# A two-layer hybrid mixer network on one core: a list schedule that books the SBUF port, with priorities for each part of each mixer

## The chip, the core and the metric

The kernel runs on one core of a Trainium2 chip. The engines have short names in the rows: PE is TensorE (matmuls), PEld its weight loads, DVE is VectorE, ACT is ScalarE, POOL is GpSimd, SP is SyncE, on whose queue all transfers are issued. The metric is the device time of one execution in microseconds.

## What is computed

One inference step of a two-layer network on 384 tokens of width 1024 (128 context tokens and 256 latent tokens, which share the weights). Each layer is a half-step feed-forward block, a mixer and a second half-step feed-forward block:

```
x += 1/2 * gate1 * SwiGLU(adaLN1(RMSNorm(x)))
x += gate2 * W_out[ RWKV7 | windowed GQA+sink | gated DeltaNet ](W_in adaLN2(RMSNorm(x)))
x += 1/2 * gate3 * SwiGLU(adaLN3(RMSNorm(x)))
```

The mixer projects the normed tokens with W_in and hands the columns to three branches: RWKV7, a linear recurrence with a low-rank decay (in both directions), attention over a window of 128 with a sink and a cached context, and gated DeltaNet, a second recurrence in both directions, behind a convolution over 5 tokens:

```
S = (S * w_t[:, :, None, :]
     + jnp.einsum('bhvk,bhk->bhv', S, a_t)[..., None] * b_t[:, :, None, :]
     + v_t[..., None] * k_t[:, :, None, :])
```

Both recurrences are computed in chunks, which needs the inverse of a triangular matrix for each chunk, head and direction. Outputs are the tokens, the new keys and values, and the final states of both recurrences.

## The kernel before

**How the work is tiled.** Activations stand with channels on the 128 partitions and the 384 tokens (386 with two columns for the norm's shift) along the free axis. Every large product has float32 weights split in two: `split_w` (L940) writes whi on ScalarE and the rest wlo = wr − whi on VectorE, and `mm3` (L952) issues three matmuls of 128x128 by 128x386 for each pair. The feed-forward products are pg, pu and po, the mixer's input projections are pw (`project`, L1060: a product, then `evac`, which reads it out of PSUM with rstd into pg and on into prj); the mixer's output projection w_out is called po as well (po2 in the code, shown as po in the trace).

**The mixer** (L1037) is written in parts, each with a label: prR (projections of the RWKV branch), preR (decays and scan inputs kr, kt, bt, and the products lr), inv0 (the inverse for RWKV), prD (projections and convolution cv of the delta branch), gates, unit, prA (projections of attention), lev0 (assembling larger blocks of the inverse), preD, inv1 (the inverse for the delta branch), lev1, attnp and attn0 to attn2, and the scans scR and scD, for two groups of heads, three chunks and two directions each. A scan step is a short chain between PE, ScalarE and VectorE (yu, U, sd, btk, pd, ks). At the end of a scan comes a norm over heads (its mean is bm) and a product with a gate, which gives y, the input of the output projection.

`stage_inv` (L1299) works through 31 columns; each is a product `pr = R * Z` and a subtraction `Z -= pr` on 112 partitions, so a chain of 62 operations in a row, which may stand on VectorE or on GpSimd. Their widths go from 31 up to 256 and down again.

**What sets the order.** Nothing is issued as it is written. A `Recorder` (L198) notes every operation with what it depends on. `estimate` (L376) gives each a duration, `order` (L426) then plays the program through: whenever an engine is free, the ready operation with the highest priority goes. The priority `cp` is the longest way to the end of the program in modelled time, plus a bias by label from `BIAS`, plus 5000 for an accumulation that has begun. Operations recorded by `any`, `tt`, `copy`, `scale` or `fill` have several engines to choose from (`alts`); an engine that is free passes such an operation when another would have it done over 60 ns sooner, by the model. On PE, an operation whose weight tile has another shape than the last is put off as long as one of the same shape is at most `near` less urgent. Where the modelled PE would not be dense enough, the planner emits a filler, a 128x128 matmul on zeros (idle_ps, L706). `issue` (L695) then writes the operations in that order; most rows of the trace bear its line, L718. The order on each engine is fixed from there on; at run time an engine waits in that order for what it needs.

Of the kernel before, what the change touches and what calls it, by code (L numbers as in the profile page):

```python
# [36 lines left out]
SIDE = ("vvvvv", "mmm", "vvvv", "vvvv", "", "")  # L37

ROOM = {"kA": "h", "kS": "h", "vt": "h", "pt": "h", "ev": "h", "w0b": "h", "lora": "h", "yb": "r"}
TUNE = {'near': 2000.0, 'ahead': 8000.0, 'ahead2': 8000.0, 'finish': 5000.0, 'clock': True, 'dummy': 53.5, 'd1': 3600.0, 'd2': 7000.0}  # L40

BIAS = {'ada02': -100000.0, 'ada03': -100000.0, 'ada04': -100000.0, 'ada05': -100000.0, 'ada06': -100000.0, 'ada07': 0.0, 'ada08': 0.0, 'ada10': 0.0, 'ada11': -100000.0, 'ada12': -100000.0, 'ada13': -100000.0, 'ada14': -100000.0, 'ada15': -100000.0, 'ada16': -100000.0, 'ada17': -100000.0, 'ada18': -100000.0}
PLACES = {"u": 30, "r": 3, "w": 6, "a": 3, "b": 2, "h": 5, "t": 10, "ps": 7, "mxs": 2, "dram_ada": 2, "dram_s1": 2, "dram_s2": 2, "dram_s3": 2, "s4": 6}


# [123 lines left out]
class Op:  # L169
    __slots__ = ("eng", "meth", "args", "kw", "cost", "lat", "preds", "succs", "bufs", "idx", "cp", "need", "ready",  # L170
                 "start", "end", "tset", "label", "group", "seed", "filler", "follows", "pos", "held", "stall", "dma", "alts", "done",
                 "name", "real", "parts", "seq", "lead", "mode", "out")


class _Eng:
# [22 lines left out]
class Recorder:  # L198
# [91 lines left out]
    def any(self, *choices):  # L290

        op = self.add(*choices[0][:2], (), choices[0][2])
        op.alts = {}
        for eng, meth, kw in choices:
            op.eng, op.meth, op.kw = eng, meth, kw
            self.estimate(op)
            op.alts[eng] = (meth, kw, op.cost, op.lat, op.tset)
        self.choose(op, min(op.alts, key=lambda e: op.alts[e][2]))
        return op

    def choose(self, op, e):
        op.eng = e
        op.meth, op.kw, op.cost, op.lat, op.tset = op.alts[e]

    def copy(self, out, in_, pool=True):
        c = [("scalar", "copy", dict(out=out, in_=in_)), ("vector", "tensor_copy", dict(out=out, in_=in_))]
# [69 lines left out]
    def estimate(self, op):  # L376
# [4 lines left out]
        views = [v for v in list(a) + list(kw.values()) if isinstance(v, View)]  # L381
        ps = any(v.buf.tag in PSUM for v in views)
        sc = sum(isinstance(kw.get(k), View) for k in ("scalar", "scalar1", "scalar2", "bias", "scale", "accum_out"))
        op.tset, op.dma = None, 0.0
        e, m = op.eng, op.meth
        if m == "dma_start":
            nbytes = n * out.shape[0] * 4
            run = min(v.shape[-1] for v in (out, kw["in_"])) * 4
# [2 lines left out]
        elif e == "tensor":  # L391
            op.lat = 200.0
            op.seq = [self.product(*p) for p in op.parts]
            op.held = sum(p[3] for p in op.seq)
            op.cost = self.stream(0.0, op.seq, [0.0] * 16, 1.0)[1]
            op.mode, op.out = op.seq[0][4], op.seq[-1][4]
        elif e == "vector":
            if m == "tensor_reduce":
                n = int(np.prod(kw["in_"].shape[1:]))
            if m == "reciprocal":  # L400
                n *= 6
            full = ps or m in ("stream_shuffle", "tensor_reduce", "reciprocal") or any(k in kw for k in ("in1", "data"))
            op.cost = (65 + (n if full else n / 2)) / 0.96 + 62 * sc
            if m == "memset":
                op.cost = 8 + n
            op.lat = 130.0
        elif e == "scalar":
            op.cost = ((61 if isinstance(kw["in_"], View) and kw["in_"].buf.tag in PSUM else 112) + n) / 1.2 + 93 * sc
            op.tset = TSETS.get(kw.get("func"))
            op.lat = 142.0  # L410
        else:
            op.cost = 130 + n * (4.3 if sc else 3.3)
            if m == "memset":
                op.cost = 35 + n * 0.83
            elif m == "tensor_tensor":
                op.cost = 150 + n * 2.1
            elif m == "scalar_tensor_tensor":
                op.cost = 95 + n * 1.39
            op.lat = 120.0

    def wait(self, op, o):
        if op.eng == "tensor" and o.eng == "tensor":
# [3 lines left out]
    def order(self):  # L426
# [79 lines left out]
        def enter(op):  # L506
# [4 lines left out]
            else:  # L511
                heapq.heappush(gated, (op.pos - (self.ahead2 if op.follows else self.ahead), op.idx))

        win, busy, over, warm, ndum, past, dens, colt = 0, 0.0, 0.0, False, 0, [], 0.0, [0.0] * 16
        mode, nsw = (P, P), 0
        bus, tset, now, out, emit, wake, stuck = 0.0, None, 0.0, [], [], [], False
        for op in ops:
            if op.need == 0:
                enter(op)
        while len(out) < len(ops):  # L520
# [10 lines left out]
            for e in engs:  # L531
# [6 lines left out]
                while avail[e]:  # L538
# [15 lines left out]
                        op.stall = tag  # L554
                        continue
                    if op.alts:
                        here, best = now + op.alts[e][2], 1e18
                        for f in op.alts:
                            if f != e:
                                queue = sum(ops[x[1]].cost for x in avail[f] if x < item and not ops[x[1]].done)  # L560
                                best = min(best, max(free[f], now) + queue + op.alts[f][2])
                        if best < here - 60:
                            passed.append(item)
                            continue
# [86 lines left out]
                if op.tset and op.tset != tset:  # L651
                    tset = op.tset
                    cost += 1300.0
                op.start = now
                free[e] = now + cost
                if e != "tensor":
# [1249 lines left out]
```

## Time and profile before

| | us |
|---|---|
| median of 3 runs (1887.55 to 1890.82) | 1888.9 |
| profiled execution | 1892.28 |
| its span | 1890.5 |

| engine | busy us | share of the span |
|---|---|---|
| PE | 1842.2 | 97% |
| DVE | 1336.9 | 71% |
| ACT | 856.4 | 45% |
| POOL | 206.2 | 11% |

The page gives for the chain of work that ended last: PE 82% of the span, DVE 8%, ACT 4%, POOL 2%, DMA 2%. In time, the span is: feed-forward block to 345 us, first mixer (mixer 0) to 660, two feed-forward blocks to 1255, second mixer (mixer 1) from 1280 to 1575, feed-forward block to the end. A row of a timeline groups neighbouring instructions of one form (x4); its first number is the start in us from the start of the span, its second the duration, and a bracket gives the idle time before it and what ended it. PEclk is the clock granted to PE as a share of full speed.

### The profile page before, as it was taken

Reading aid. Unit: us, or ns where it says so; the run is one execution under the profiler, and the core shown is the slowest. Engines: PE = TensorE matmul, PEld = TensorE weight load, DVE = VectorE, ACT = ScalarE, POOL = GpSimd, SP = SyncE. Lnnn points to the kernel's source line nnn. Section 1 sums busy time; section 2 is a strip of 40 time slices with the busy share of each in tenths; the row PEclk is TensorE's granted clock in tenths of the full one; section 3 lists DMA queues with packets and bytes.
Section 4 is the critical chain, followed back from the end, with each engine's and each line's share of the span. In section 5 each row is a group of like instructions: output and inputs, shape, how many; then the busy total and the mean of one; then the engine's idle time right before and its main releaser. Section 6 shows DMA issues by size and latency. Waiting matters only on the chain.

```text
span 1890.5 us, 34461 instructions
## 1 busy us (share of the span) xinstructions
PE 1842.2 (97%) x13589; PEld 1690.1 (89%) x13589; DVE 1336.9 (71%) x2680; ACT 856.4 (45%) x1777; POOL 206.2 (11%) x322
## 2 busy tenths in 40 slices
PE   8999999989999999999999999998899999999998
PEld 6999999778766799999999999997686679999998
DVE  3999954886775679995459995458879646555444
ACT  4444433657445454443344443347664444434323
POOL 0000000251320200000000000014525011000000
PEclk9999999999899999999999999999999999999999
DMA  9566644365421255664455664443341213434442
GB/s 363 200 222 230 241 137 164 124 196 157 109 46 39 78 205 203 216 241 126 125 201 206 214 243 126 126 137 91 79 102 42 66 52 101 123 123 123 128 123 84
DMA packets 144033, 279.46 MB, mean 148 GB/s; under 512 B 50192, under 2 KB 76880, under 8 KB 143872
## 3 DMA queue, kind: packets, MB, share of 16 engines
q1 hardware_dynamic: 143872, 277.26, 46.1%
q8 instruction: 107, 1.75, 0.4%
q14 instruction: 54, 0.44, 0.1%
HBM read 264.80 MB, written 11.89 MB: 146 GB/s over the span
## 4 chain that ended last, share of the span: by engine, by line
PE 82%; DVE 8%; ACT 4%; POOL 2%; DMA 2%; issue 1%; SPq 0%; DVEq 0%; ACTq 0%; POOLq 0%
PE po L718 23%; PE pg L718 20%; PE pu L718 20%; PE pw L718 5%; PE idle_ps L706 3%; POOL pr L718 1%; ACT L714 1%; POOL Z L718 1%; PE q L718 1%; PE z L718 1%; DVE mxs L718 1%; PE gram L718 1%; PE pr L718 1%; PE aps L718 1%; PE sc L718 1%
## 5 line engine op out<-in xcount | busy, mean ns | idle before, releaser
L718 DVE TENSOR_TENSOR wlo<-wr,whi 128x1024 fp32r<-128x1024 f32 (+2 forms) x334 | 400.8, 1203 | 90.4 <-ACT whi L718 90.1
L718 ACT CAST whi<-wr 128x1024 fp32r<-128x1024 f32 (+2 forms) x334 | 339.7, 1019 | 174.4 <-PE po L718 84.4
L718 PE MATMUL pg<-xs,whi 128*128 128x386 f32 x1408 | 366.3, 341 | 0.2 <-POOL xs L718 0.2
L718 PE MATMUL pu<-xs,whi 128*128 128x386 f32 x1408 | 365.8, 341 | 0.0
L718 PE MATMUL po<-h,whi 128*128 128x384 f32 x1408 | 360.1, 337 | 0.0
L718 PEld LDWEIGHTS pg<-xs,whi 128*128 128x128 f32 x1408 | 257.4, 189 | 0.9 <-POOL xs L718 0.5
L718 PEld LDWEIGHTS pu<-xs,whi 128*128 128x128 f32 x1408 | 257.4, 189 | 0.0
L718 DVE CUSTOM_DVE_ANT_0 unread<-arow,crow 128x1024 bf16<-128x1024 f32 x208 | 253.8, 1220 | 3.0 <-ACT crow L718 1.1
L718 PEld LDWEIGHTS po<-h,whi 128*128 128x128 f32 x1408 | 255.7, 188 | 0.0
L718 PE MATMUL pu<-xs,wlo 128*128 128x386 f32 x704 | 238.8, 339 | 0.6 <-DVE wlo L718 0.6
L718 PE MATMUL pg<-xs,wlo 128*128 128x386 f32 x704 | 238.7, 339 | 0.0
L718 PE MATMUL po<-h,wlo 128*128 128x384 f32 x704 | 237.4, 337 | 0.0
L718 PE MATMUL pw<-xs,whi 128*128 128x386 f32 (+1 forms) x736 | 198.4, 350 | 9.8 <-ACT whi L718 7.1
L718 DVE SCALAR_TENSOR_TENSOR xT<-po,mods,xT 128x256 f32<-128x256 f32 (+1 forms) x96 | 35.3, 413 | 169.4 <-PE po L718 169.2
L718 PEld LDWEIGHTS pw<-xs,whi 128*128 128x128 f32 (+1 forms) x736 | 131.7, 186 | 21.3 <-ACT whi L718 8.6
L718 PE MATMUL pw<-xs,wlo 128*128 128x386 f32 (+1 forms) x368 | 128.4, 350 | 7.8 <-DVE wlo L718 7.6
L718 PEld LDWEIGHTS pu<-xs,wlo 128*128 128x128 f32 x704 | 134.1, 190 | 1.1 <-DVE wlo L718 1.1
L718 PEld LDWEIGHTS pg<-xs,wlo 128*128 128x128 f32 x704 | 134.1, 190 | 0.5 <-DVE wlo L718 0.4
L718 PEld LDWEIGHTS po<-h,wlo 128*128 128x128 f32 x704 | 132.1, 188 | 0.0
L706 PEld LDWEIGHTS <-idle_z 128*128 128x128 bf16 x1553 | 96.1, 100 | 33.2 <-issue 26.6
L706 PE MATMUL idle_ps<-idle_z 128*128 128x128 bf16 x1553 | 123.4, 224 | 0.0
L718 ACT CAST h<-up 128x384 fp32r<-128x384 f32 x88 | 45.2, 514 | 151.0 <-DVE up L718 151.0
(363 smaller groups left out, 2466.1 us busy)
## 6 DMA issues: line engine op xcount, KB each, us to landing
wr<-in_ffn_in SPq DMA_DIRECT2D x176, 512.0 KB, 4.5
arow<-in_adat SPq DMA_DIRECT2D x104, 512.0 KB, 3.6
wr<-in_ffn_out SPq DMA_DIRECT2D x64, 512.0 KB, 3.7
wr<-in_w_in SPq DMA_DIRECT2D x44, 512.0 KB, 4.5
wr<-in_ffn_out SPq DMA_DIRECT2D x32, 384.0 KB, 3.3
araw<-in_ada SPq DMA_DIRECT2D x24, 512.0 KB, 5.2
araw<-in_ada SPq DMA_DIRECT2D x32, 256.0 KB, 6.5
wr<-in_w_out SPq DMA_DIRECT2D x16, 512.0 KB, 4.0
```

Source lines behind the costliest of these rows:

```text
L706: self.nc.tensor.matmul(ps[:, 0:n], lhsT=z[:, 0:P], rhs=z, start=True, stop=True)
L714: self.nc.scalar.preload_act_table_set(cur)
L718: ins = getattr(getattr(self.nc, op.eng), meth)(*[fix(x) for x in args], **{k: fix(x) for k, x in kw.items()})
```

## The change

What is computed stays the same. Four things change in the planner:

- `near` goes from 2000 to 500.
- `BIAS` loses three entries that were 0 and gets 18 for parts of one mixer each; a label with .0 or .1 at its end is the part in mixer 0 or 1, and 1000 is 1 us of urgency.
- Operations of VectorE with sources in SBUF and all operations of GpSimd get a `port`: 1 for a fill of GpSimd, 2 for its other operations and for those of VectorE with two sources in SBUF, 3 for VectorE's with one. `turn` gives the time at which such an operation could begin when the one on the other engine has ended; a started operation is booked as longer by that wait, and the choice between engines counts it.
- Durations in `estimate` are corrected: fills, VectorE's tensor_tensor_reduce and copies on 112 partitions, GpSimd's products of one column and other operations.

```diff
-TUNE = {'near': 2000.0, 'ahead': 8000.0, 'ahead2': 8000.0, 'finish': 5000.0, 'clock': True, 'dummy': 53.5, 'd1': 3600.0, 'd2': 7000.0}
+TUNE = {'near': 500.0, 'ahead': 8000.0, 'ahead2': 8000.0, 'finish': 5000.0, 'clock': True, 'dummy': 53.5, 'd1': 3600.0, 'd2': 7000.0}
...
+    "ada11": -100000.0, "ada12": -100000.0, "ada13": -100000.0, "ada14": -100000.0, "ada15": -100000.0,
+    "ada16": -100000.0, "ada17": -100000.0, "ada18": -100000.0, "attn0.0": -500.0, "attn1.1": -2100.0,
+    "attn2.1": -11300.0, "attnp.0": 11700.0, "attnp.1": -12600.0, "inv1.1": -16600.0, "prA.1": 900.0,
+    "prR.0": -500.0, "prR.1": 2700.0, "preD0.0": 12800.0, "preD0.1": 14800.0, "preD1.1": -1400.0, "preR1.1": 3200.0,
+    "scD0.1": 900.0, "scD1.0": 4700.0, "scD1.1": 3400.0, "scR1.1": 1300.0, "unit.1": -800.0}
...
+            elif m == "tensor_tensor_reduce":
+                op.cost = 65 / 0.96 + n / 0.96
+            elif not full and out.shape[0] == 112:
+                op.cost = (65 + n) / 0.96
...
-            op.cost = 130 + n * (4.3 if sc else 3.3)
+            op.cost = 480 + n * (4.3 if sc else 3.3)
...
+                op.cost = 165 + n * 2.1 if n > 1 else 450.0
...
+        if e == "vector" and not ps and m not in ("stream_shuffle", "reciprocal", "tensor_reduce", "memset"):
+            op.port = 2 if src == 2 else 3
+        elif e == "gpsimd":
+            op.port = 1 if m == "memset" else 2
...
+        def turn(e, kind, t):
+
+            x = port["gpsimd" if e == "vector" else "vector"] if kind else (0.0, 0.0)
+            if kind == 1:
+                return max(t, x[1])
+            return max(t, x[0], x[1] if kind == 3 else 0.0)
...
-                        here, best = now + op.alts[e][2], 1e18
+                        here, best = turn(e, op.alts[e][5], now) + op.alts[e][2], 1e18
...
-                                best = min(best, max(free[f], now) + queue + op.alts[f][2])
+                                best = min(best, turn(f, op.alts[f][5], max(free[f], now)) + queue + op.alts[f][2])
...
+                if op.port:
+                    cost += turn(e, op.port, now) - now
+                    if op.port == 1:
+                        port[e][1] = now + cost
+                    else:
+                        port[e][0] = now + cost
+                        if op.port == 3:
+                            port[e][1] = now + cost
```

In the order of all instructions, the fillers go from 1553 to 1373: in the projection part of mixer 0 from 69 to 107, in its scan part from 483 to 273, in mixer 1 from 102 to 203 and from 493 to 347, between the mixers from 85 to 115, ahead of the first from 217 to 224. Changes of tile shape on PE go from 577 to 484. Of the operations with a choice, 157 go from GpSimd to VectorE and 97 the other way, 159 from VectorE to ScalarE and 96 the other way. The first inverse has 35 steps on GpSimd and 31 on VectorE before and 17 and 49 after in mixer 0, 41 and 25 before and 15 and 50 after in mixer 1 (with its fills).

VectorE in the projection part of mixer 1, inside the first inverse; cv are steps of the convolution, pg reads a projection out of PSUM, wlo splits weights. Before:

```order
L718 TENSOR_TENSOR wlo_13917<-wr_13850,whi_13901 128x1024
L718 TENSOR_TENSOR Z_13482<-Z_13482,pr_13825 112x24x8
L718 SCALAR_TENSOR_TENSOR cv_13925<-prj_13752,vecs_80,cv_13925 128x386
L718 SCALAR_TENSOR_TENSOR cv_13881<-prj_13496,vecs_80,cv_13881 128x386
L718 SCALAR_TENSOR_TENSOR cv_13925<-prj_13752,vecs_80,cv_13925 128x386
L718 TENSOR_TENSOR pg_13949<-pw_13893,rstd_13104 128x384
L718 SCALAR_TENSOR_TENSOR cv_13925<-prj_13752,vecs_80,cv_13925 128x386
L718 TENSOR_TENSOR Z_13482<-Z_13482,pr_13825 112x22x10
L718 SCALAR_TENSOR_TENSOR cv_13925<-prj_13752,vecs_80,cv_13925 128x386
L718 TENSOR_TENSOR wlo_13974<-wr_13911,whi_13954 128x1024
```
After:

```order
L749 TENSOR_TENSOR Z_13366<-Z_13366,pr_13847 112x24x8
L749 SCALAR_TENSOR_TENSOR cv_13963<-prj_13377,vecs_80,cv_13963 128x386
L749 TENSOR_TENSOR pr_13847<-R_13362,Z_13366 112x207
L749 SCALAR_TENSOR_TENSOR cv_13995<-prj_13773,vecs_80,cv_13995 128x386
L749 TENSOR_TENSOR Z_13366<-Z_13366,pr_13847 112x23x9
L749 SCALAR_TENSOR_TENSOR cv_13995<-prj_13773,vecs_80,cv_13995 128x386
L749 TENSOR_TENSOR wlo_14016<-wr_13974,whi_14006 128x8x16
L749 TENSOR_TENSOR pr_13847<-R_13362,Z_13366 112x220
L749 SCALAR_TENSOR_TENSOR cv_13950<-prj_13773,vecs_80,cv_13950 128x386
L749 TENSOR_TENSOR Z_13366<-Z_13366,pr_13847 112x22x10
```
Between two steps Z of VectorE before lie many others, and the pr between them are on GpSimd; after, pr and Z come in turn on VectorE, with a cv between.

GpSimd at the same place. Before:

```order
L718 TENSOR_TENSOR pr_13825<-R_13469,Z_13482 112x175
L718 TENSOR_TENSOR Z_13482<-Z_13482,pr_13825 112x25x7
L718 TENSOR_TENSOR pr_13825<-R_13469,Z_13482 112x192
L718 TENSOR_TENSOR pr_13825<-R_13469,Z_13482 112x207
L718 TENSOR_TENSOR Z_13482<-Z_13482,pr_13825 112x23x9
L718 TENSOR_TENSOR pr_13825<-R_13469,Z_13482 112x220
L718 TENSOR_TENSOR pr_13825<-R_13469,Z_13482 112x231
```
After:

```order
L749 TENSOR_TENSOR pr_13847<-R_13362,Z_13366 112x31
L749 TENSOR_TENSOR pr_13847<-R_13362,Z_13366 112x135
L749 TENSOR_TENSOR Z_13366<-Z_13366,pr_13847 112x27x5
L749 TENSOR_TENSOR pr_13847<-R_13362,Z_13366 112x175
L749 TENSOR_TENSOR pr_13847<-R_13362,Z_13366 112x192
L749 TENSOR_TENSOR pr_13847<-R_13362,Z_13366 112x247
L749 TENSOR_TENSOR Z_13366<-Z_13366,pr_13847 112x18x14
```
Before, GpSimd had nearly every pr of the widening half of the chain, and about every other Z; after, it has single steps, with gaps in their widths where VectorE has the steps.

PE at the end of mixer 1, in the last steps of the second delta scan; po are products of the output projection, two by two for whi and one for wlo, idle_ps is the filler. Before:

```order
L718 MATMUL yu_17153<-dvp_17125,Y_16382 64x64 x4
L718 MATMUL sd_17158<-U_16857,tok_14264 64x64 x2
L718 MATMUL btk_17161<-cst_78,bt_13652 128x128
L718 MATMUL btk_17161<-cst_78,kt_13713 128x128
L706 LDWEIGHTS idle_z
L706 MATMUL idle_ps<-idle_z 128x128
L706 LDWEIGHTS idle_z
L706 MATMUL idle_ps<-idle_z 128x128
L718 MATMUL btk_17171<-cst_78,bt_13652 128x128
L718 MATMUL pd_16853<-D_14974,U_17163 64x128 x2
L718 MATMUL btk_17171<-cst_78,kt_13713 128x128
```
After, from the last product ahead of the last bm on:

```order
L749 MATMUL po_2869_17018<-y_15996,wlo_16986 128x384
L749 MATMUL bm_17048<-ds_17022,cst_78 128x384
L749 MATMUL po_2863_16888<-y_17042,whi_16858 128x384
L749 MATMUL po_2869_17018<-y_17042,whi_16970 128x384
L749 MATMUL po_2875_17058<-y_16788,whi_17034 128x384 x2
L749 MATMUL po_2875_17058<-y_16788,wlo_17046 128x384
L749 MATMUL po_2875_17058<-y_16790,whi_17034 128x384 x2
L749 MATMUL po_2863_16888<-y_17042,whi_16858 128x384
L749 MATMUL po_2863_16888<-y_17042,wlo_16884 128x384
L749 MATMUL po_2863_16888<-y_16087,whi_16858 128x384 x2
```
Before, the chain's last steps stand alone with fillers between them, since the po products went ahead in long batches (rows before these); after, products of po are left over for the time behind bm.

## Rows read from the trace of the kernel before

**Rows 1.** The page, part 1: busy time by engine.

```profile
PE 1842.2 (97%) x13589; PEld 1690.1 (89%) x13589; DVE 1336.9 (71%) x2680; ACT 856.4 (45%) x1777; POOL 206.2 (11%) x322
```

**Rows 2.** Busy time, clock and transfers by stretch of the span.

```profile
core 0: us, PE busy (x) PEld busy (x) DVE busy (x) ACT busy (x) POOL busy (x), PEclk, DMA share, GB/s
...
350.00:470.00 120.00, 107.32 (x668) 85.59 (x667) 92.92 (x192) 81.59 (x161) 49.40 (x63) 0.96 0.54 160
470.00:660.00 190.00, 185.45 (x2440) 134.59 (x2439) 132.68 (x399) 87.52 (x246) 37.47 (x51) 0.97 0.26 67
670.00:1250.00 580.00, 580.00 (x3332) 578.71 (x3332) 439.48 (x755) 237.47 (x430) 5.85 (x14) 1.00 0.56 185
1280.00:1395.00 115.00, 101.41 (x779) 86.32 (x780) 88.95 (x172) 76.72 (x160) 48.80 (x65) 0.96 0.40 101
1395.00:1575.00 180.00, 174.44 (x2253) 128.89 (x2251) 125.01 (x378) 82.94 (x230) 43.16 (x66) 0.98 0.21 52
```

**Rows 3.** By stretch, the fillers (tile idle_ps) alone: busy, count, clock.

```profile
350.00:470.00 120.00, 6.04 (x69) 0.96 0.54 160
470.00:660.00 190.00, 41.83 (x483) 0.97 0.26 67
1280.00:1395.00 115.00, 8.35 (x111) 0.96 0.40 101
1395.00:1575.00 180.00, 40.07 (x488) 0.98 0.21 52
```

**Rows 4.** Timeline of PE, end of mixer 1: start, us, what, idle before.

```profile
1566.21 0.86 PE L718 MATMUL bm<-ds,cst 128*128 128x384 f32 x2
1566.91 2.62 PE L706 MATMUL idle_ps<-idle_z 128*128 128x128 bf16 x44
1569.94 0.80 PE L718 MATMUL po<-y,whi 128*128 128x384 f32 x3 [0.41 <-DVE y L718]
```

**Rows 5.** Timeline of PE, mixer 1, a change of tile shape.

```profile
1551.29 0.51 PE L718 MATMUL po<-y,whi 128*128 128x384 f32 x2
1551.64 0.34 PE L718 MATMUL po<-y,wlo 128*128 128x384 f32 x1
1551.91 0.34 PE L718 MATMUL sd<-U,tok 128*64 128x64 f32 x4
```

**Rows 6.** Timeline of GpSimd (POOL), mixer 1, two steps of one shape.

```profile
1328.13 1.98 POOL L718 TENSOR_TENSOR pr<-R,Z 112x207 f32<-112x207 f32 x1 [0.47 <-DVE Z L718]
...
1353.59 0.55 POOL L718 TENSOR_TENSOR pr<-R,Z 112x207 f32<-112x207 f32 x1 [2.74 <-DVE Z L718]
```

**Rows 7.** Timeline of VectorE (DVE), mixer 1.

```profile
1327.97 1.68 DVE L718 SCALAR_TENSOR_TENSOR cv<-prj,vecs,cv 128x386 f32<-128x386 f32 x3
...
1352.20 0.40 DVE L718 TENSOR_TENSOR Z<-Z,pr 112x231 f32<-112x231 f32 x1
```

**Rows 8.** Waits of PE, 1294 to 1352: total us, times, longest.

```profile
PE pw L718 <- DVE wlo L718: 6.0, 5, 2.0
PE pw L718 <- ACT whi L718: 2.4, 2, 1.4
PE pw L718 <- ACT s L718: 1.8, 1, 1.8
```

**Rows 9.** Waits of PE, 366 to 432.

```profile
PE pw L718 <- ACT whi L718: 4.5, 2, 4.2
PE lr L718 <- DVE bt L718: 3.6, 2, 2.5
```

**Rows 10.** Stretches of low clock; columns as in group 2.

```profile
373.00:380.00 7.00, 5.81 (x41) 3.40 (x37) 7.00 (x10) 2.93 (x11) 5.65 (x6) 0.52 0.44 138
...
506.50:516.50 10.00, 10.00 (x76) 6.39 (x73) 8.44 (x31) 3.41 (x14) 2.04 (x4) 0.50 0.30 100
1298.00:1302.00 4.00, 3.91 (x34) 3.50 (x36) 4.00 (x7) 2.46 (x7) 3.12 (x4) 0.57 0.21 63
...
sum 38.50, PE 34.21 PEld 22.40 DVE 34.54 ACT 16.36 POOL 21.28; mean PE 5.70 PEld 3.73 DVE 5.76 ACT 2.73 POOL 3.55
```

More of the change, by code (lines that the diff above doesn't have):

```diff
@@ L39 @@
 ROOM = {"kA": "h", "kS": "h", "vt": "h", "pt": "h", "ev": "h", "w0b": "h", "lora": "h", "yb": "r"}
-TUNE = {'near': 2000.0, 'ahead': 8000.0, 'ahead2': 8000.0, 'finish': 5000.0, 'clock': True, 'dummy': 53.5, 'd1': 3600.0, 'd2': 7000.0}
-BIAS = {'ada02': -100000.0, 'ada03': -100000.0, 'ada04': -100000.0, 'ada05': -100000.0, 'ada06': -100000.0, 'ada07': 0.0, 'ada08': 0.0, 'ada10': 0.0, 'ada11': -100000.0, 'ada12': -100000.0, 'ada13': -100000.0, 'ada14': -100000.0, 'ada15': -100000.0, 'ada16': -100000.0, 'ada17': -100000.0, 'ada18': -100000.0}
+TUNE = {'near': 500.0, 'ahead': 8000.0, 'ahead2': 8000.0, 'finish': 5000.0, 'clock': True, 'dummy': 53.5, 'd1': 3600.0, 'd2': 7000.0}
+BIAS = {"ada02": -100000.0, "ada03": -100000.0, "ada04": -100000.0, "ada05": -100000.0, "ada06": -100000.0,
[5 rows of a table added]
 PLACES = {"u": 30, "r": 3, "w": 6, "a": 3, "b": 2, "h": 5, "t": 10, "ps": 7, "mxs": 2, "dram_ada": 2, "dram_s1": 2, "dram_s2": 2, "dram_s3": 2, "s4": 6}
@@ L171 @@
                  "start", "end", "tset", "label", "group", "seed", "filler", "follows", "pos", "held", "stall", "dma", "alts", "done",
-                 "name", "real", "parts", "seq", "lead", "mode", "out")
+                 "name", "real", "parts", "seq", "lead", "mode", "out", "port")
 class _Eng:
@@ L296, in any @@
             self.estimate(op)
-            op.alts[eng] = (meth, kw, op.cost, op.lat, op.tset)
+            op.alts[eng] = (meth, kw, op.cost, op.lat, op.tset, op.port)
         self.choose(op, min(op.alts, key=lambda e: op.alts[e][2]))
@@ L302, in choose @@
         op.eng = e
-        op.meth, op.kw, op.cost, op.lat, op.tset = op.alts[e]
+        op.meth, op.kw, op.cost, op.lat, op.tset, op.port = op.alts[e]
     def copy(self, out, in_, pool=True):
@@ L383, in estimate @@
         sc = sum(isinstance(kw.get(k), View) for k in ("scalar", "scalar1", "scalar2", "bias", "scale", "accum_out"))
-        op.tset, op.dma = None, 0.0
+        op.tset, op.dma, op.port = None, 0.0, 0
         e, m = op.eng, op.meth
+        src = sum(isinstance(kw.get(k), View) for k in ("in_", "in0", "in1", "data"))
         if m == "dma_start":
@@ L404, in estimate @@
             if m == "memset":
-                op.cost = 8 + n
+                op.cost = 10 + n * 0.79
+            elif m == "tensor_tensor_reduce":
+                op.cost = 65 / 0.96 + n / 0.96
+            elif not full and out.shape[0] == 112:
+                op.cost = (65 + n) / 0.96
             op.lat = 130.0
@@ L411, in estimate @@
         else:
-            op.cost = 130 + n * (4.3 if sc else 3.3)
+            op.cost = 480 + n * (4.3 if sc else 3.3)
             if m == "memset":
-                op.cost = 35 + n * 0.83
+                op.cost = 50 + n * 0.84
             elif m == "tensor_tensor":
-                op.cost = 150 + n * 2.1
+                op.cost = 165 + n * 2.1 if n > 1 else 450.0
             elif m == "scalar_tensor_tensor":
@@ L516, in order @@
         bus, tset, now, out, emit, wake, stuck = 0.0, None, 0.0, [], [], [], False
+        port = {"vector": [0.0, 0.0], "gpsimd": [0.0, 0.0]}
         for op in ops:
```

## The prediction

> **What bounds the kernel now.** I read the page's busy line first, then the table by stage, and then, only in the stages with holes, the waits of TensorE (PE), its fillers and its clock. The busy line [rows 1] says PE 97%, so the kernel is bound by PE, and a change of order pays only where PE is idle, does idle work, changes its tile shape or runs at a lower clock. The stage table [rows 2] tells where that is. The feed-forward stretch is solid, 580.00 of 580.00 us at clock 1.00: no order can win there. The two mixers are not. I call their first parts, in which the input projections run, the projection stages (350 to 470 and 1280 to 1395), and the rest the scan stages (470 to 660 and 1395 to 1575). PE is not busy for 120.00 − 107.32 = 12.7 us, 4.6 us, 13.6 us and 5.6 us of these four, 36 us together. And part of what counts as busy is idle matmuls, the fillers: 69, 483, 111 and 488 of them [rows 3]. One filler takes 2.62 us / 44 = 0.06 us [rows 4], so 1151 of them are 69 us. Bare holes plus fillers are 105 us; tile shapes and clock come on top. That is all that the change can touch.
>
> **Why the holes are there.** In the projection stages PE waits for weights and scan inputs. Between 1294 and 1352 it waits 6.0 us in 5 times for VectorE's wlo, 2.4 us for ScalarE's whi and 1.8 us for its copy s [rows 8]; between 366 and 432 it waits 4.5 us for whi and 3.6 us for VectorE's bt [rows 9]. Behind them stands a contention that the old planner does not know: a GpSimd product pr of 112x207 takes 1.98 us in one place and 0.55 us in another [rows 6], and the slow one spans three cv steps of VectorE that end back to back after 1.68 us [rows 7]; it gets going when they are through. So VectorE and GpSimd take turns on data in SBUF, and the old plan is wrong where both work. The planner thought that wlo, bt and the inverse would be there earlier, put no filler, and PE stood. Shortly after such places the granted clock is at 1.2 GHz: six stretches of 38.5 us in all at 0.50 to 0.57, with 34.21 us of PE work in them [rows 10].
>
> **The change part by part.** I count fillers and tile-shape changes in the two orders, and take times from rows.
>
> Fillers of the scan stages: 483 become 273 in mixer 0 and 493 become 347 in mixer 1, 356 fewer. At 0.06 us this is **−21 us**. The order shows what replaces them: in mixer 1, between the last delta steps, products po of the output projection now stand where fillers stood, and the mean bm that needed 44 fillers behind it [rows 4] is now followed by more than a dozen po products that are ready. The bounds are 0 (the products that fill the holes are missing elsewhere, and PE waits there bare) and −21.
>
> Projection stages: holes and fillers today are 26.3 us + 180 × 0.06 = 37.1 us. The new plan has 107 + 203 = 310 fillers there, 18.6 us, because it now sees waits that used to come as a surprise. If its view were perfect, these fillers would be all that is left: −18.5 us. If nothing improved and the added 130 fillers stood before the same waits, they would cost up to +8 us. I take **−8.5 us**, that is 18.6 us of fillers and 10 us of holes. The value lies between for two reasons. GpSimd loses work: its steps of the first inverse go from 35 to 17 in mixer 0 and from 41 to 15 in mixer 1, the rest on VectorE, where a step of 112x231 takes 0.40 us [rows 7], against 1.98 us for 112x207 on a GpSimd that has to wait [rows 6]. But about 32 steps stay on GpSimd in this stretch, and the row shows the slow one waiting through several VectorE instructions, not one.
>
> On that point a rule speaks about the change itself. The Trainium skill, "SBUF — State Buffer", section "SBUF: two separate sides", says that the pair of ports shared by VectorE and GpSimd is an exclusive lock, held for the whole instruction by whichever starts first, with the other blocked until then. Taken as strict turns, which is how the new planner books it, GpSimd would get in after at most one cv, the plan would be right, and the projection term would be its far end, −18.5 us; the row with three cv steps in one wait says that a turn can be lost to the next instruction, which is why I stay at about half of it.
>
> VectorE's load: the first inverses bring it 18 + 25 = 43 steps, 43 × 0.40 = 17 us in both projection stages. It is idle there for 120.00 − 92.92 = 27.1 us and 115.00 − 88.95 = 26.1 us [rows 2], which hides 7 and 10 us; beside that, 159 operations leave VectorE for ScalarE and 96 come back, and ScalarE is idle for 38 us in each of the two stages [rows 2]. Nothing is charged; without that cover it is 17 us.
>
> Tile-shape changes: PE goes from 577 to 484. The smaller "near" alone would make the planner readier to change (a matmul of the present shape may now be only 500 less urgent, not 2000, to go first); the new priorities of the parts outweigh it in the count. A po product follows the next after 0.35 / 2 = 0.175 us, but the small sd follows the last po after 0.27 us [rows 5]: 0.095 us for a change. 93 × 0.095 = **−9 us**; the other end is 0, where PE would have waited anyway.
>
> Clock: the work in the six slow stretches is 34.21 us [rows 10], at full clock 17 us, so at most −17 us. As the contention episodes get rarer but don't go, I take a third, **−6 us**; the other end is 0, and below that stands a rival.
>
> Fillers elsewhere: 85 to 115 between the mixers and 217 to 224 at the start, 37 × 0.06 = **+2 us**.
>
> New waits: with fewer fillers the plan has less slack for what it gets wrong. The scan stages have 4.6 + 5.6 = 10.2 us of bare holes today [rows 2]; I add half, **+5 us**, with ends of 0 and +15 (one and a half times today's on top).
>
> The sum: −21 − 8.5 − 9 − 6 + 2 + 5 = −37.5 us. The profiled execution took 1892.3 us, so 1854.8 by it; it lies 3.4 us above the median of 1888.9, and so the forecast for the median is 1851.4, say **1852 us**.
>
> **The rivals.** *All of it comes true:* strict turns, no new waits, the slow clock stretches nearly gone: −21 − 18.5 − 9 − 15 + 2 = −61.5, about 1827 us. For it: most of the big holes name wlo, whi or bt, just what the new model books later. Against it: the GpSimd row above.
>
> *Only the counts pay:* the waits of the projection stages and the clock stay, the added fillers come on top by half: −21 + 4 − 9 + 2 + 5 = −19, so 1870 us. For it: ScalarE's whi and s are in the lists too, and the port says nothing on these; VectorE could also be late by the 17 us of inverse steps, with the same outcome.
>
> *Nothing moves:* the removed fillers stood in waits of the serial chains of the scans (the fillers behind bm fill a wait for VectorE's y [rows 4]), and PE waits for the same results without them. The scan stages then keep their length, and added fillers eat what the tile shapes give: about 1887 us. Against it: the new order puts products there, and each of these is missing later, where PE was full.
>
> *The clock falls, and it is slower:* fillers are there to keep PE dense. With 356 fewer, in stages where PE today runs at 0.97 and 0.98 [rows 2], stalls that the plan doesn't see would find less work around them. Work of a us at full clock takes two at 1.2 GHz; so 75 us of the 370 us of the scan stages at the low clock, which hold 37 us of work, eat the whole forecast gain. From there it is slower; at 95 us it adds 47 us, 1899 us. For it: 506.5 to 516.5, where PE was busy for all of 10.00 us and yet at clock 0.50 [rows 10], just after a wait in the scan stage. Against it: the places of the fillers are filled with larger products, which are denser work.
>
> **How the numbers follow.** Forecast 1852 us: 0.46. All of it (1827): 0.17. Only the counts (1870): 0.19. Nothing moves (1887): 0.06. Clock (1899): 0.12. A measurement of this kernel can tell about 0.2%, 3.8 us, from no change. The first three cases are faster by more than that: 0.82; same: 0.06; slower: 0.12. For 8 in 10 the range leaves out the slower half of the last two cases and the faster half of the second: 1826 to 1887 us.
>
> **What would show it.** Right: in the scan stages 600 to 650 fillers and a PE span shorter by over 15 us together; in the projection stages holes of less than 20 us together; waits of PE for wlo below 3 us in mixer 1; GpSimd rows of 112-wide steps near 0.55 us, few above 1.2; slow clock stretches of 20 to 30 us together; the feed-forward stretch unchanged. Wrong: a stretch of tens of us at clock 0.5 in the scan stages (the clock rival), waits of PE for VectorE's Z or pr at the start of the scans (the load on VectorE was not hidden), or scan stages with fewer fillers but as long as before (the chains set the end, not PE).

## The result and the profile after

| | before | after |
|---|---|---|
| median, us | 1889.9 | 1838.8 |
| ratio | | 0.974, 95% interval 0.972 to 0.976 |
| profiled execution | 1892.28 | 1838.75 |
| its span | 1890.5 | 1836.9 |

The changed kernel is 51 us faster, 1852 had been forecast. The page's busy line of after answers to [rows 1]; the same order of reading serves again.

```profile
PE 1806.4 (98%) x13409; PEld 1670.5 (91%) x13409; DVE 1308.2 (71%) x2677; ACT 877.3 (48%) x1840; POOL 144.0 (8%) x261
```

PE is busy for 35.8 us less, on the same matmuls but for the fillers; GpSimd lost 62 us of work. The stretches of after, to be read as [rows 2], are cut at the first pw of a mixer, at its last pw and at the first product of the block that follows:

```profile
320.70:460.40 139.70, 137.30 (x874) 115.64 (x874) 110.53 (x228) 96.03 (x192) 29.15 (x52) 1.00 0.60 183
460.40:643.10 182.70, 178.80 (x2344) 137.35 (x2343) 138.94 (x408) 105.00 (x291) 40.12 (x59) 0.99 0.30 80
650.00:1210.00 560.00, 556.54 (x3216) 552.81 (x3215) 423.86 (x732) 228.30 (x413) 0.40 (x4) 1.00 0.55 184
1216.70:1347.90 131.20, 130.14 (x882) 118.94 (x881) 101.09 (x216) 96.58 (x189) 31.29 (x53) 1.00 0.39 109
1347.90:1542.70 194.80, 187.90 (x2406) 145.03 (x2403) 140.24 (x412) 107.40 (x299) 38.87 (x66) 0.97 0.27 70
```

The four mixer stretches of before, cut the same way:

```profile
318.50:470.60 152.10, 139.38 (x849) 115.72 (x849) 114.60 (x230) 98.47 (x194) 49.40 (x63) 0.97 0.54 164
470.60:678.60 208.00, 203.45 (x2544) 152.84 (x2544) 147.14 (x426) 97.10 (x264) 40.93 (x57) 0.98 0.28 74
1245.70:1391.90 146.20, 132.94 (x817) 116.43 (x818) 112.12 (x212) 93.33 (x190) 54.26 (x88) 0.96 0.39 105
1391.90:1595.10 203.20, 197.19 (x2518) 151.33 (x2517) 144.20 (x414) 96.36 (x260) 48.12 (x72) 0.98 0.24 63
```

So the projection stages gave 12.4 and 15.0 us, the scan stages 25.3 and 8.4 us, together 61 us, and the feed-forward blocks and the start took 7.5 us back. The bare holes of the two projection stages, 12.72 + 13.26 = 26.0 us before, are now 139.70 − 137.30 = 2.4 and 131.20 − 130.14 = 1.1, 3.5 us together. In mixer 1, the list of PE's waits that was [rows 8] for part of the stage is now, for all of it:

```profile
PE tokp L749 <- DVE sh L749: 0.4, 1, 0.4
PE abp L749 <- ACT abT L749: 0.3, 1, 0.3
```

No wait for wlo is left there. The fillers by stage (columns as in [rows 3]):

```profile
320.70:460.40 139.70, 7.71 (x107) 1.00 0.60 183
460.40:643.10 182.70, 22.84 (x273) 0.99 0.30 80
1216.70:1347.90 131.20, 13.65 (x203) 1.00 0.39 109
1347.90:1542.70 194.80, 29.94 (x347) 0.97 0.27 70
```

At the end of mixer 1 the chain that ended last shows what replaced them (start, duration, what): behind the last bm stand 162 po products without a break, where [rows 4] had 44 fillers and a hole.

```profile
1511.07 2.82 PE po L749 x15
1513.89 0.65 PE bm L749 x2
1514.53 28.33 PE po L749 x162
```

The stretches at the low clock, to be read as [rows 10], are three instead of six, 15.5 us instead of 38.5:

```profile
465.00:469.00 4.00, 4.00 (x50) 3.62 (x36) 1.94 (x8) 1.86 (x6) 0.00 (x0) 0.57 0.65 181
1352.50:1360.00 7.50, 7.22 (x145) 6.34 (x138) 4.29 (x17) 6.05 (x17) 0.00 (x0) 0.54 0.19 53
1393.00:1397.00 4.00, 4.00 (x46) 3.37 (x44) 2.89 (x12) 3.28 (x18) 1.63 (x3) 0.57 0.02 6
```

### The profile page after: what moved, and what is told of

Same layout as the page of the kernel before. It is cut to its first block, busy times and chain, and to the rows that moved or that the text cites. A ratio compares the mean times of both kernels' runs of the same rounds, so it can differ in the third digit from the quotient of the medians.

```text
span 1836.9 us, 34056 instructions
## 1 busy us (share of the span) xinstructions
PE 1806.4 (98%) x13409; PEld 1670.5 (91%) x13409; DVE 1308.2 (71%) x2677; ACT 877.3 (48%) x1840; POOL 144.0 (8%) x261
## 4 chain that ended last, share of the span: by engine, by line
PE 60%; DVE 23%; ACT 6%; DMA 5%; issue 4%; SPq 1%; POOL 0%; DVEq 0%; POOLq 0%; ACTq 0%
PE po L749 24%; PE pg L749 9%; PE pu L749 9%; DVE unread L749 8%; DVE wlo L749 6%; PE pw L749 4%; DMA wr<-in_ffn_in 3%; DVE up L749 3%; PE idle_ps L737 2%; ACT whi L749 1%; ACT L745 1%; PE q L749 1%; DVE cv L749 1%; PE sc L749 1%; PE gram L749 1%
## 5 line engine op out<-in xcount | busy, mean ns | idle before, releaser
L749 PE MATMUL pw<-xs,whi 128*128 128x386 f32 (+1 forms) x736 | 194.2, 345 | 2.0 <-ACT s L749 1.5
L737 PEld LDWEIGHTS <-idle_z 128*128 128x128 bf16 x1373 | 82.8, 98 | 25.9 <-issue 20.3
L737 PE MATMUL idle_ps<-idle_z 128*128 128x128 bf16 x1373 | 104.1, 221 | 0.0
```

Source lines behind the costliest of these rows:

```text
L737: self.nc.tensor.matmul(ps[:, 0:n], lhsT=z[:, 0:P], rhs=z, start=True, stop=True)
L749: ins = getattr(getattr(self.nc, op.eng), meth)(*[fix(x) for x in args], **{k: fix(x) for k, x in kw.items()})
```

## The experiments

Two theories were to be told apart. Theory A: the booked turns at the SBUF port take the bare holes out of the projection stages, and the other gains follow the counts of fillers and tile-shape changes. Rival B: the denser order does it, whatever the planner books. "Holes" below is PE's idle time in the two projection stages, cut as above. "Low clock" is the time at half clock, worked out from the mean granted clock of a profiled run, which is recorded to three digits; so it is good to some 2 us, and it holds for that one execution.

**1. One part alone, and two without the port.** `near_only` and `bias_only` put one part of the change into the kernel before, the new near (below) or the 18 new priorities:

```diff
-TUNE = {'near': 2000.0, ...
+TUNE = {'near': 500.0, ...
```

> The kernel before with near 500 alone: old priorities, no port in the planner. Its order has 1418 fillers (135 fewer than before) and 536 changes of tile shape (before 568, after 475, counted the same way). Theory A (the booked turns at the port remove the bare holes of the projection parts and the low-clock stretches; fillers and tile shapes pay by their count): only the counts pay, 135 x 0.06 + 32 x 0.1 = 11 us, so 1879 us, with 20 us or more of bare holes left in the two projection parts and about 35 us at low clock. Rival B (the holes go because the order is denser, whoever books what): holes below 12 us together and 1865 us or less.

Measured: 1879.7 us, ratio 0.994 (0.992 to 0.996); holes 24.3 us, as Theory A said. The three other executions lie at 1875 to 1880 us, the profiled one at 1890, with 60 us at low clock.

> The kernel before with the new priorities of the mixer parts alone. 1502 fillers (51 fewer than before), 547 changes of tile shape. Theory A (port removes holes): 3 + 2 = 5 us by the counts, 1885 us, holes of the projection parts as before, 20 us or more. Rival B (the priorities carry the gain, the port little): 1860 us or less, holes below 12 us.

Measured: 1892.0 us, ratio 1.002 (1.000 to 1.003); holes 26.5 us. The holes stay, as Theory A said; its time was 7 us too low.

`port_only` is the changed planner (durations and turns) with the old near and priorities:

> The kernel before with the planner's new durations and turns alone, near 2000 and old priorities. 2194 fillers (641 more than before), 585 changes of tile shape. Theory A (the turns remove holes and low clock, fillers cost 0.06 us each wherever they stand): the holes of the projection parts fall below 8 us together, the low-clock stretches below 20 us; time 1890 + 641 x 0.06 - 20 - 11 = 1897 us. Rival C (most of the added fillers only show waits that the engines had anyway): 1875 us or less. Rival B (the port does nothing): holes as before, 1928 us.

Measured: 1903.4 us, ratio 1.007 (1.005 to 1.008). The part that removes the holes makes the kernel slower on its own. Its projection stages:

```profile
320.40:468.80 148.40, 143.43 (x946) 119.48 (x945) 113.23 (x243) 102.97 (x202) 25.47 (x38) 1.00 0.61 184
1253.20:1400.50 147.30, 140.83 (x1043) 126.63 (x1043) 112.84 (x234) 98.03 (x195) 24.48 (x48) 1.00 0.40 105
```

5.0 + 6.5 = 11.5 us of holes where less than 8 were expected, and 7.6 us at low clock; 641 more fillers, 328 of them in the projection stages, cost more than that gives. Theory A's time was 6 us too low; B (1928) and C (1875) are out.

`no_port` keeps near and the priorities of the change and loses durations and turns (only the cut of the turns is shown):

```diff
...
-            op.port = 2 if src == 2 else 3
-        elif e == "gpsimd":
-            op.port = 1 if m == "memset" else 2
+            op.port = 0
```

> The changed kernel without the planner's new durations and turns: near 500 and the new priorities stay. 1755 fillers, 538 changes of tile shape. Theory A: holes of the projection parts are back at 20 us or more, low-clock stretches at 30 us or more; by the counts 1890 + 202 x 0.06 - 3 = 1899 us. Rival B (priorities and near carry the gain): 1860 us or less.

Measured: 1909.7 us, ratio 1.010 (1.008 to 1.012), 11 us above Theory A's time. The holes are back:

```profile
316.80:465.10 148.30, 136.96 (x800) 114.83 (x800) 114.17 (x215) 92.71 (x186) 51.45 (x74) 0.95 0.51 154
1261.00:1406.90 145.90, 130.78 (x746) 116.65 (x745) 108.24 (x217) 93.70 (x183) 53.07 (x80) 0.95 0.38 103
```

11.3 + 15.1 us, and first in PE's waits in mixer 1 stands wlo again:

```profile
PE pw L743 <- DVE wlo L743: 6.9, 8, 1.3
```

From the traces so far a sum emerged: span = 1669 us + 0.058 us per filler + 0.11 us per change of tile shape + all bare holes of PE + half of the low-clock time. The prices of a filler and a shape change are those of the prediction, the constant is what is left over.

**2. One part taken away.** `no_bias` is the changed kernel with the old priorities, `no_near` with near 2000:

> The changed kernel with the old priorities: near 500, new durations and turns stay. 1775 fillers (changed kernel 1373), 569 changes of tile shape (475). From the runs so far a time adds up as 1669 us + 0.058 us per filler + 0.11 us per change of tile shape + PE's bare holes + half of the low-clock time; plans that book the turns have about 33 us of holes in the whole span and 4 to 7 us from the clock, plans that don't have 50 and 27. So Theory A: 1669 + 103 + 63 + 33 + 6 = 1874 us, holes of the projection parts below 12 us. Rival B (the booked turns only help with the new priorities): holes 20 us or more, 1890 us or more.

Measured: 1874.4 us, holes 2.8 us, ratio to before 0.992 (0.990 to 0.995). The executions lie between 1867 and 1881; the profiled one, 1880.2, has 33.8 us at low clock, which cost it 17 us where 6 were expected. The median met the expectation, the clock did not.

> The changed kernel with near back at 2000. 1917 fillers, 566 changes of tile shape. Theory A: 1669 + 111 + 62 + 33 + 6 = 1881 us, holes of the projection parts below 12 us. Rival B (a lower near is what removes the holes): 20 us or more of holes there, 1900 us or more.

Measured: 1879.6 us, holes 5.7 us, ratio 0.995 (0.994 to 0.997). Theory A's time was right to 1.4 us.

`turn_off` keeps the new durations and drops the ports (the diff shown for no_port alone), `cost_back` drops the new durations and keeps the ports:

> The changed kernel with the new durations, but no operation has a port, so that no turns are booked; near 500 and the new priorities stay. 1949 fillers, 550 changes of tile shape. Theory A (the turns are what removes the holes, not the corrected durations): holes of the projection parts 20 us or more, 1669 + 113 + 61 + 51 + 27 = 1921 us. Rival D (the corrected durations do it): holes below 12 us, 1882 us.

Measured: 1925.4 us, ratio 1.019 (1.017 to 1.021), holes 24.2 us. Rival D, that the corrected durations remove the holes, fell.

> The changed kernel with the old durations; the turns are booked, near 500 and the new priorities stay. 1700 fillers, 596 changes of tile shape. Theory A (booking turns is enough to take the holes out of the projection parts): holes there below 12 us, 1669 + 99 + 66 + 33 + 6 = 1873 us. Rival D (it takes the corrected durations too): 20 us or more of holes, 1900 us or more.

Measured: 1868.0 us, ratio 0.988 (0.985 to 0.991), holes 7.6 us, 5 us below Theory A's time. Booking the turns is enough to bring the holes below 12 us; with the corrected durations as well they are 3.5 us.

**3. The inverses on VectorE alone.** `before_inv_dve` is the old kernel, planner and all, with one thing changed: the steps of the inverses may not go to GpSimd. The planner then makes a new order around them.

```diff
-                nc.tt(p3, R[:, 0:c, c:c + 1]...
-                nc.tt(Z[:, 0:c, c:32], Z[:, 0:c, c:32], p3, ALU.subtract)
+                nc.vector.tensor_tensor(out=p3, in0=R[:, 0:c, c:c + 1]...
+                nc.vector.tensor_tensor(out=Z[:, 0:c, c:32], in0=Z[:, 0:c, c:32], in1=p3, op=ALU.subtract)
```

> The kernel before, in which the 62 steps of every inverse are bound to VectorE; planner, near and priorities as before. 1537 fillers (before 1553), 567 changes of tile shape. Theory A (the holes of the projection parts come from GpSimd and VectorE working at once in the inverse, which the old plan doesn't book): holes there from 26 us to 12 us or less, little time at low clock; 1669 + 89 + 62 + 37 + 5 = 1862 us. Rival F (they come as much from the scan inputs kr, kt and bt, which stay on both engines): holes of 18 us or more, 1885 us or so.

Measured: 1868.1 us, ratio 0.988 (0.986 to 0.990): 22 us faster than before by two lines. Its projection stages:

```profile
319.00:463.10 144.10, 137.03 (x852) 115.33 (x852) 117.42 (x259) 94.89 (x191) 22.58 (x30) 0.99 0.61 181
1225.00:1364.90 139.90, 130.78 (x862) 116.92 (x863) 113.89 (x247) 93.14 (x191) 24.02 (x50) 1.00 0.42 107
```

The holes are 7.1 + 9.1 = 16.2 us, between the 12 of Theory A and the 18 of rival F. In mixer 1, the wait for wlo is nearly gone, but those for whi and bt stay:

```profile
PE pw L718 <- ACT whi L718: 4.3, 3, 1.6
PE lr L718 <- DVE bt L718: 2.0, 2, 1.1
PE pw L718 <- DVE wlo L718: 0.9, 1, 0.9
```

So the inverse on two engines is behind not quite half of the holes that the change removes, 10 of 22.5 us. Most of the low clock went with it: 7.5 of 38 us are left in the profiled executions, 11 of 27 us by the mean clock of all executions on record. The rest of the holes sits in waits that this edit doesn't reach. Whether the gain comes from the contention or from the chain no longer crossing between two engines, of which GpSimd takes 0.55 us for a step of 112x207 even undisturbed [rows 6] and VectorE 0.40 for one of 112x231 [rows 7], is not told apart by this run. VectorE is busy for only 2.8 and 1.8 us more than before in these stages, although it does some 70 steps that GpSimd did there; what gives that time back was not taken apart.

**4. The clock rival.** `after_thin` is the changed kernel without any filler:

```diff
-'d1': 3600.0, 'd2': 7000.0}
+'d1': 0.0, 'd2': 0.0}
```

> The changed kernel with no fillers at all (both limits of the planner for them at 0); 442 changes of tile shape (475). This is the rival of the prediction on the clock taken to its end. If the fillers only stand where PE waits anyway, their 80 us become bare holes; if the clock then falls for 60 us or more, the time is above 1839: 1669 + 49 + 113 + 30 = 1861 us. If fillers delay the work behind them and the clock holds, the holes stay near 50 us and the time is about 1770 to 1800 us.

Measured: 1874.7 us, ratio to before 0.992 (0.990 to 0.994), so 36 us slower than the changed kernel and 14 us above the 1861 expected. The low-clock stretches add up to 116 us, PE's holes in the whole span to 90 us. The longest low-clock stretches:

```profile
509.00:534.00 25.00, 14.61 (x75) 9.16 (x77) 21.91 (x68) 7.26 (x25) 3.10 (x5) 0.52 0.17 45
1400.00:1422.00 22.00, 20.77 (x117) 14.63 (x117) 17.77 (x58) 8.95 (x34) 11.51 (x16) 0.53 0.29 66
1489.00:1524.00 35.00, 32.96 (x479) 24.32 (x478) 15.74 (x52) 18.06 (x49) 0.00 (x0) 0.51 0.01 2
```

The rival's mechanism is real and its price as large as was said; the change just doesn't go that far. In the one place shown, behind the last bm of mixer 1, products stand where its missing fillers stood.

The projection stages of after_thin say something more:

```profile
322.40:466.80 144.40, 133.07 (x772) 110.39 (x771) 111.21 (x227) 93.66 (x193) 28.07 (x53) 0.99 0.57 171
1236.10:1375.20 139.10, 127.81 (x684) 111.50 (x685) 104.56 (x232) 97.07 (x199) 28.34 (x50) 0.95 0.39 109
```

The turns are booked, and yet there are 11.3 + 11.3 = 22.6 us of bare holes. So part of what left the list of holes in the changed kernel was filled and not removed; how large a part is worked out below, from the counts.

**5. How far the priorities carry.** `nudge` is the changed kernel with one priority moved by 0.1 us:

```diff
-    "attn0.0": -500.0
+    "attn0.0": -400.0
```

> The changed kernel with one priority moved by a tenth of a us: attn0.0 from -500 to -400. 1460 fillers (changed kernel 1373), 539 changes of tile shape (475). Theory A with the counts: 1669 + 85 + 59 + 33 + 6 = 1852 us, 13 us slower than the changed kernel, which would say that the gain of the priorities is that of one plan among many and not that of any one entry. Rival E (the entries matter by their size): within 2 us of 1839.

Measured: 1852.7 us, ratio to before 0.981 (0.980 to 0.983), so 14 us behind the changed kernel, as the counts said; rival E fell. In mixer 0's scan stage it has 358 fillers instead of 273:

```profile
460.80:659.40 198.60, 32.45 (x358) 0.99 0.26 71
```

`tuned` moves seven priorities further for fewer fillers:

> The changed kernel with seven of its priorities moved further (inv1.1 -19600, preD1.1 -2400, scD0.1 -100, scD1.1 3000, unit.1 2200, scR0.0 3000, prD.0 -300), chosen for an order with fewer fillers. 1334 fillers (changed kernel 1373), 461 changes of tile shape (475). By the counts 39 x 0.058 + 14 x 0.11 = 4 us less: 1835 us if holes (30 us) and clock stay as in the changed kernel. Rival: new holes at other places eat it, 1839 us or more.

Measured: 1839.9 us, ratio to before 0.973 (0.970 to 0.975), the same as the changed kernel, so the rival and not the 1835 us expected: 39 fillers fewer, and the holes of the whole span grow from 30.5 to 35.5 us. No version beat the changed kernel.

**The sum over all fourteen kernels.** Holes here are those of the whole span, in us; the second number is that of the projection stages.

| kernel | median | fillers | shape changes | holes | low clock | sum | span |
|---|---|---|---|---|---|---|---|
| before | 1889.9 | 1553 | 568 | 48.3 / 26.0 | 37.8 | 1889 | 1890.5 |
| near_only | 1879.7 | 1418 | 536 | 50.8 / 24.3 | 60.4 | 1891 | 1888.4 |
| bias_only | 1892.0 | 1502 | 547 | 53.5 / 26.5 | 53.0 | 1896 | 1891.9 |
| no_port | 1909.7 | 1755 | 538 | 52.7 / 26.5 | 53.5 | 1909 | 1909.5 |
| turn_off | 1925.4 | 1949 | 550 | 58.0 / 24.2 | 34.6 | 1918 | 1924.6 |
| before_inv_dve | 1868.1 | 1537 | 567 | 39.8 / 16.2 | 7.5 | 1864 | 1866.6 |
| port_only | 1903.4 | 2194 | 585 | 36.2 / 11.4 | 7.6 | 1901 | 1900.7 |
| cost_back | 1868.0 | 1700 | 596 | 31.3 / 7.6 | 3.7 | 1866 | 1866.0 |
| no_bias | 1874.4 | 1775 | 569 | 27.9 / 2.8 | 33.8 | 1879 | 1878.4 |
| no_near | 1879.6 | 1917 | 566 | 30.6 / 5.7 | 7.5 | 1877 | 1878.0 |
| nudge | 1852.7 | 1460 | 539 | 33.4 / 3.2 | 7.4 | 1850 | 1850.3 |
| after | 1838.8 | 1373 | 475 | 30.5 / 3.5 | 14.7 | 1839 | 1836.9 |
| tuned | 1839.9 | 1334 | 461 | 35.5 / 2.6 | 14.7 | 1840 | 1837.0 |
| after_thin | 1874.7 | 0 | 442 | 89.6 / 22.6 | 115.7 | 1865 | 1866.1 |

Fillers and shape changes are counted in the orders, holes and clock in the traces; shape changes here are counted between operations, which for the kernel before gives 568 where the prediction's count between matmuls gave 577 (the difference between before and after is 93 by both). The sum meets the span of the profiled execution within 7 us in all fourteen, and within 3 us in twelve. It is bookkeeping, with a constant set by the first traces; that it also holds for the kernels that came after is what speaks for the prices in it. Every plan that books the turns and has fillers has less than 12 us of holes in the projection stages; every plan that doesn't book them, and leaves the inverse to both engines, has over 24.

But a hole that gets a filler costs PE nearly the same time. Holes and fillers (at 0.058 us each) of the projection stages together are the better measure, counted in the traces: 36 us before, 40 in port_only, 32 in no_port, 34 in turn_off, 27 in cost_back, 21.5 in the changed kernel. So of the 22.5 us of holes that the changed kernel lost, 14.4 are gone and 8 are filled. Against turn_off the booked turns shorten the idle time itself by some 12 us; in port_only they shorten nothing and only put fillers where the planner now sees the waits. Whether they do it by the choice between the engines or by the times that the planner counts with was not tried.

## Why the prediction was right

The direction, the bound (PE) and most of the mechanism held; the forecast was short by 13 us. Of the signs that it named, two missed: the low-clock stretches are 15.5 us where 20 to 30 were said, and the feed-forward stretch did change. Term by term, each as forecast and as measured by the sum above:

| term | forecast | measured |
|---|---|---|
| fillers of the scan stages, 356 fewer | −21 | −21 |
| projection stages, holes and fillers | −8.5 | −14.4 |
| changes of tile shape, 93 fewer | −9 | −10 |
| clock | −6 | −11.5 |
| fillers elsewhere | +2 | +2 |
| new waits | +5 | +4.7 |
| sum | −37.5 | −50 |

The spans differ by 53.6 us; 3.5 us stay outside these terms.

*Projection stages.* This term was mis-sized. The step that failed is "18.6 us of fillers and 10 us of holes": the fillers came as counted, but only 3.5 us of holes stayed (26.0 − 3.5 = 22.5 us less, against 139 × 0.058 = 8.1 us more in fillers). The reason given for staying at half was that a GpSimd step can lose several turns in a row [rows 6, 7]. The traces bear that reading out, and more widely than the prediction knew. In the kernel before, seven steps of the inverse on GpSimd took 1.98 to 2.29 us, and each was kept out by two or three VectorE instructions that followed each other. The first of them, a Z, waits for a cv and a wlo, and then gets in beside a pg, which reads PSUM:

```profile
402.10 2.04 POOL L718 TENSOR_TENSOR Z<-Z,pr 112x192 f32<-112x192 f32 x1 [0.77 <-DVE pr L718]
...
401.95 0.61 DVE L718 SCALAR_TENSOR_TENSOR cv<-prj,vecs,cv 128x386 f32<-128x386 f32 x1
402.48 1.21 DVE L718 TENSOR_TENSOR wlo<-wr,whi 128x1024 fp32r<-128x1024 f32 x1
403.61 0.54 DVE L718 TENSOR_TENSOR pg<-pw,rstd 128x384 f32<-128x384 f32 x1
```

What the prediction mis-sized is how rare such steps become in the new order. Of the steps of the inverse that the traces show on GpSimd, 11 of 107 took longer than 1.2 us before and 3 of 70 after, none of them over 1.51 us. The two longer ones in mixer 1 and two ordinary ones, in the timeline of GpSimd, and the wlo of VectorE beside the second:

```profile
1312.10 1.36 POOL L749 TENSOR_TENSOR pr<-R,Z 112x247 f32<-112x247 f32 x1 [7.95 <-DVE Z L749]
...
1315.67 1.51 POOL L749 TENSOR_TENSOR pr<-R,Z 112x255 f32<-112x255 f32 x1
...
1327.58 0.57 POOL L749 TENSOR_TENSOR pr<-R,Z 112x220 f32<-112x220 f32 x1
...
1331.04 0.53 POOL L749 TENSOR_TENSOR pr<-R,Z 112x192 f32<-112x192 f32 x1 [2.88 <-DVE Z L749]
...
1315.15 1.52 DVE L749 TENSOR_TENSOR wlo<-wr,whi 128x1024 fp32r<-128x1024 f32 x1
```

At 1315.67 VectorE is in a wlo that takes 1.52 us from 1315.15, so this is one turn lost, not three. The Trainium skill ("SBUF — State Buffer", section "SBUF: two separate sides") has the port locked by one instruction at a time. These rows agree with the lock; they don't agree with strict turns, which the planner books and which put the term at its far end of −18.5 us. The measured −14.4 lies nearer to that far end than to the forecast. That this comes from the few steps left in which GpSimd could lose a turn is read from these rows; no run isolates it.

*Clock.* A third of 17 us was taken, and in the profiled executions 38 us at low clock became 15, which is the −11.5 of the table. But the profiled execution of before lies at the low end. By the mean granted clock of all executions, 0.993 in the 36 of before that ran beside the experiments and 0.995 in the four of the changed kernel, it is 27 and 17 us, and the term is −5 us, close to the forecast; some 7 us of the gain in the median then lie outside the terms. It is the loosest of them: no_bias has hardly a hole in its projection stages, and 34 us at low clock in its profiled execution.

*New waits.* Right in size, wrong in place, so the size was luck. The scan stages have 10.8 us of holes where they had 10.6, despite the 356 fillers fewer. Instead the feed-forward stretch, which I had called solid and out of reach, has 3.5 us, and the start 1.0 us more. Between 640 and 800 us PE waits for wlo:

```profile
PE pg L749 <- DVE wlo L749: 1.4, 1, 1.4
PE pu L749 <- DVE wlo L749: 0.8, 2, 0.4
```

The runs show which part of the change brings this, though not how: the corrected durations. The feed-forward stretch between the mixers lasts 566 to 568 us in all six kernels with the old durations and 571 to 574 in all eight with the corrected ones, whatever else they have. cost_back (turns, old durations) and turn_off (no turns, corrected durations), this stretch:

```profile
664.20:1231.40 567.20, 566.93 (x3258) 565.10 (x3258) 429.13 (x737) 232.43 (x419) 0.53 (x8) 1.00 0.57 186
714.30:1287.00 572.70, 570.09 (x3290) 567.07 (x3289) 429.26 (x736) 232.70 (x419) 2.87 (x4) 1.00 0.57 185
```

So the corrected durations, with which holes and fillers of the projection stages go from 27 us (cost_back) to 21.5, cost some 5 us here.

*The rivals.* "Only the counts pay" fell: the projection stages gave 14.4 us where it has them cost 4. "Nothing moves" fell: 356 fillers fewer made the scan stages 33.6 us shorter. The clock rival was shown to exist in after_thin. VectorE's 43 added steps were hidden: its busy time in the projection stages fell, from 114.6 and 112.1 us to 110.5 and 101.1.

*What the prediction did not see.* It added the parts up as if each paid by itself. The medians of the eight combinations of near, priorities and planner say otherwise: none 1889.9, near 1879.7, priorities 1892.0, planner 1903.4, near and priorities 1909.7, near and planner 1874.4, priorities and planner 1879.6, all three 1838.8. Alone, the three sum to some +5 us; together they give −51. The counts already said so: the plan with everything has 1373 fillers, and the other combinations have 1418 to 2194. The prediction was right since it counted in the order that was to run, not in its parts. Why the three fit together is not shown; that nudge loses 14 us by a tenth of a us in one priority suggests that the priorities suit just this planner and this near, and say little outside of them.

## What to carry to other kernels

When a planner sets the order, cost a change in the finished order (idle work, shape changes, places where two engines share a port) and not by the entries of its tables: one priority moved by 0.1 us was worth 14 us here. When a wait looks like a late weight, see what else held up the engine that makes it: here it was, in part, GpSimd's share in a serial chain, and giving that to VectorE in two lines was worth 22 us under the old plan. When holes vanish from a trace, count the fillers that came in their place: of 22.5 us here, 8 were filled and only 14.4 were gone. A better model can make things slower alone, as port_only did; with the near and the priorities of the change the same planner gave the fastest order here.

## What the runs showed of the hardware

The low clock can last while PE is busy throughout. In near_only it held for 24 us in which PE had no hole at all; in the 10 us ahead, at full clock, PE had been idle for 0.79 us:

```profile
596.00:606.00 10.00, 9.21 (x295) 7.18 (x291) 6.12 (x17) 5.96 (x17) 0.00 (x0) 1.00 0.02 4
606.00:630.00 24.00, 24.00 (x218) 20.04 (x218) 3.77 (x12) 5.14 (x13) 0.00 (x0) 0.50 0.01 1
```

Executions of one kernel differ along with this. The four of near_only took 1890.2, 1880.0, 1879.4 and 1875.3 us at mean granted clocks of 0.984, 0.992, 0.993 and 0.995; the six of no_bias go from 1880.8 us at 0.993 and 1880.2 at 0.991 to 1867.2 at 0.999; those of no_near, at 0.997 and 0.998, stay within 1.4 us. The profiled execution of no_bias, at 0.991, has a stretch of 24 us at half clock; an execution at 0.999 has less than 6 us of it in all. So the same order of instructions can meet a long low stretch or miss it. What decides that was not tried.

Without fillers, PE was busy for 32.96 of 35 us and yet at 0.51 (after_thin, the last row there). And a GpSimd step of one shape takes 1.98 us beside three cv of VectorE [rows 6, 7] and 0.55 us at 1353.59, within a pause of VectorE: the same instruction at 3.6 times its time.

```profile
1354.54 0.55 DVE L718 TENSOR_TENSOR pg<-pw,rstd 16x384 f32<-16x384 f32 x1 [1.10 <-PE pw L718]
```

A pg, which reads PSUM, did not keep GpSimd out: the Z at 402.10 ran through beside one, ending at 404.14, before the pg did at 404.15.
